# The reciprocal root of the first and of the last layer norm block begun from a ScalarE table function instead of a bit trick on VectorE

## The chip, the cores and the metric

The kernel runs on one core of a Trainium2 chip. The metric is device time in microseconds (us) of one execution, lower is better; several executions are timed and their median is the kernel's time. The engines are called by the profile's short names: PE (TensorE, matrix products), PEld (its weight loads), DVE (VectorE), ACT (ScalarE), POOL (GpSimd) and SP (SyncE, which here only issues DMAs). Each engine runs its own list of instructions in order; semaphores make one wait for another.

## The reference

Two decoder layers over 512 tokens of width 1024 in float32, with a layer norm ahead of the first layer. A layer projects its input, does sliding-window and sparse attention, projects back, adds and normalizes, then does a gated feed-forward network with a gated side input, adds and normalizes again.

```python
def layer_norm(x, g, b):
    mu = x.mean(-1, keepdims=True)
    var = jnp.square(x - mu).mean(-1, keepdims=True)
    return (x - mu) * lax.rsqrt(var + LN_EPS) * g + b

def reference(x, ...):
    x = layer_norm(x, ln_in_g, ln_in_b)
    for i in range(2):
        x = hybrid_layer(x, ...)
    return x

def hybrid_layer(x, ...):
    h = x @ w_in                       # queries, keys, values, indexer
    mix = concat(window_attention, sparse_attention) @ w_o
    x = layer_norm(DN_ALPHA * x + mix, ln1_g, ln1_b)
    g, u = jnp.split(x @ w_gu, 2, axis=-1)
    ffn = (jax.nn.silu(g) * u) @ w_down
    ple = (p_i @ w_pp) * jax.nn.sigmoid(x @ w_pg)
    return layer_norm(DN_ALPHA * x + ffn + ple, ln2_g, ln2_b)
```

## The kernel before

The 512 tokens lie in four blocks of 128 rows, tiles `x0` to `x3` (in the lists of instructions they are `x_85` to `x_88`). Products are made in three passes: every operand is split into a high and a low part, and `mm3` issues the three PE instructions of lines 325, 326 and 327. Weights come by DMA into `wst`, ACT copies the high part (line 278) and POOL subtracts for the low part (line 279); both parts lie in a `wsp` tile, of which there are five.

**The reciprocal root.** `rstd_of` gives 1/sqrt(var + eps) for the 128 rows of a block. All of it runs on DVE on tiles of 128x1: line 357 makes -0.5 times the variance (`lnv`), line 358 makes the first guess by integer arithmetic on the bits (`lns`), and lines 363 and 364 are a Newton step, done three times. Every block of every norm does this, and the small norm of the indexer keys too (on 128x2).

**The start.** Block 0 of the first norm is done by `ln_in(0)`: statistics on DVE (lines 372 and 392), the deviation from the mean times the gain (line 397, two halves), the root, and the product with it (line 400, two halves). `to_features(0)` then transposes the block on PE (line 438), ACT casts the two halves into the high part `fh` (line 440) and DVE subtracts for the low part `fl` (line 441); PE multiplies with the first weights. For blocks 1 to 3 ACT makes the sums (lines 382 and 383) and the squares (line 377), DVE the rest. ACT also makes part of the table of rotary angles (six and later four instructions of line 473, two sines in lines 481 and 482) and the casts of the weights. Line 562 begins, on DVE, the indexer norm of a block from its finished product.

**The end.** The last stage makes, for one block after the other, a sigmoid on ACT (line 1031), two DVE steps (lines 1032 and 1035), the mean (line 406), the squares on ACT (line 377, whose sum is read out by a second instruction), the deviation on DVE (line 418), the root, and the last product (line 422, for the last block in three pieces), each followed by its DMA to the output (line 423).

**What sets the order.** The instructions are written in program order by the functions below, but a scheduler then puts each engine's list in an order of its own, from estimates of when each will be ready, wherever data dependencies leave it free (`schedule_with_timeline_sim=True`). A function of ACT that needs another table makes the compiler put an ACT_TABLE_LOAD ahead of it.

Of the kernel before, what the change touches and what calls it, by code (L numbers as in the profile page):

```python
# [10 lines left out]
F32 = mybir.dt.float32  # L11
F32R = mybir.dt.float32r
BF16 = mybir.dt.bfloat16
I32 = mybir.dt.int32
AF = mybir.ActivationFunctionType
OP = mybir.AluOpType

L = 2
S = 512
D = 1024  # L20
NT = S // 128
# [8 lines left out]
EPS = 1e-5  # L30
# [66 lines left out]
def hybrid_kernel(ctx: ExitStack, tc: tile.TileContext, x, p, positions, ln_in_g, ln_in_b, w_in,  # L97
# [3 lines left out]
    PE, V, A, G, SP = nc.tensor, nc.vector, nc.scalar, nc.gpsimd, nc.sync  # L101

    const = ctx.enter_context(tc.tile_pool(name="const", bufs=1))
# [9 lines left out]
    def bank(tag, bufs, dt=F32):  # L113
        return psum.tile([128, 512], dt, name="bank", tag="bank", bufs=8)

    def acc():
        return bank("acc", 4)

    def slot(dt=F32R):
        return slots.tile([128, 512], dt, name="slot", tag="slot")  # L120

    def t2k(dt=F32):
        return tmp.tile([128, 512], dt, name="t2k", tag="t2k")

    def sm(n, name):
        return small.tile([128, n], F32, name=name, tag=name)
# [192 lines left out]
    def w_rel():  # L319
        wpos["room"] += 1  # L320
        w_pump()

    def mm3(o, sh, sl, mh, ml, start, stop, again=False):

        PE.matmul(o, sh, mh, start=start, stop=False, skip_group_check=again)  # L325
        PE.matmul(o, sh, ml, start=False, stop=False, skip_group_check=again)  # L326
        PE.matmul(o, sl, mh, start=False, stop=stop, skip_group_check=again)  # L327
# [20 lines left out]
    def tok(t):  # L348
        return slice(t * 128, (t + 1) * 128)


    def rstd_of(var, n=1, of=1):

        v = sm(n, f"lnv{n}")
        s = sm(n, f"lns{n}")
        t = sm(n, f"lnt{n}")
        V.tensor_scalar(v, var, of * EPS, -0.5 / of, op0=OP.add, op1=OP.mult)
        V.tensor_scalar(s.bitcast(I32), v.bitcast(I32), -0.5, float(0x5F3759DF - 2 ** 30 - 2 ** 22),
                        op0=OP.mult, op1=OP.add)
        for _ in range(3):  # L360
            for i in range(n):
                c = slice(i, i + 1)
                V.tensor_scalar(t[:, c], s[:, c], s[:, c], v[:, c], op0=OP.mult, op1=OP.mult)
                V.tensor_scalar(s[:, c], t[:, c], 1.5, s[:, c], op0=OP.add, op1=OP.mult)
        return s
# [3 lines left out]
    def ln_stats(t, h):  # L369
        if h == 0:  # L370
            stats[t] = small.tile([128, 2, 6], F32, name="bst", tag="bst")
        V.bn_stats(stats[t][:, h, :], xt[t][:, h * 512:(h + 1) * 512])

    def squares(t, nm):

        var = sm(1, "lnvar")
        last["squares"] = A.activation(t2k().bitcast(BF16), xt[t], AF.Square, bias=nm, accum_out=var).ins
        return var
# [7 lines left out]
    def ln_in(t):  # L386
        halves = [xt[t][:, h * 512:(h + 1) * 512] for h in range(2)]
        if t == 0:
            mv = sm(2, "bmv")
            for h in range(2):  # L390
                ln_stats(t, h)
            V.bn_aggr(mv, stats.pop(t))
            mean, var, of = mv[:, 0:1], mv[:, 1:2], 1
        else:
            (mean, var), of = stats.pop(t), D
        for h, c in enumerate(halves):
            V.scalar_tensor_tensor(c, c, mean, gb_in[h], op0=OP.add if t else OP.subtract, op1=OP.mult)
        rs = rstd_of(var, of=of)
        for h, c in enumerate(halves):
            last["norm"] = V.scalar_tensor_tensor(c, c, rs, gb_in[2 + h], op0=OP.mult, op1=OP.add).ins  # L400

    def ln_sums(t, sums, key, last_norm=False):

        g_t, b_t = gb[key]
        nm = sm(1, "lnm")
        V.tensor_scalar(nm, sums[:, 0:1], sums[:, 1:2], -1.0 / D, op0=OP.add, op1=OP.mult)
        var = squares(t, nm)
        if not last_norm:
            with tc.issue_after(last["norm"]) if t == NT - 1 else nullcontext():
                V.scalar_tensor_tensor(xt[t], xt[t], nm, g_t, op0=OP.add, op1=OP.mult)  # L410
            rs = rstd_of(var, of=D)
            last["norm"] = V.scalar_tensor_tensor(xt[t], xt[t], rs, b_t, op0=OP.mult, op1=OP.add).ins
            return
        dev = []
        for h in range(2):
            c = slice(h * 512, (h + 1) * 512)
            dev.append(slot(F32))
            V.scalar_tensor_tensor(dev[h], xt[t][:, c], nm, g_t[:, c], op0=OP.add, op1=OP.mult)
        rs = rstd_of(var, of=D)
        for c0, c1 in ((0, 512), (512, D)) if t < NT - 1 else ((0, 512), (512, 768), (768, D)):  # L420
            o = dev[c0 // 512][:, c0 % 512:c0 % 512 + c1 - c0]
            V.scalar_tensor_tensor(o, o, rs, b_t[:, c0:c1], op0=OP.mult, op1=OP.add)
            SP.dma_start(out[0, t * 128:(t + 1) * 128, c0:c1], o)
# [8 lines left out]
    def to_features(t):  # L432
        ts = slice(t * 128, (t + 1) * 128)
        for j in range(KT // 4):
            ps = bank("tp", 2)
            for i in range(4):
                k = 4 * j + i
                PE.transpose(ps[:, i * 128:(i + 1) * 128], xt[t][:, k * 128:(k + 1) * 128], idf)  # L438
            pv = ps.rearrange("p (a n) -> p a n", a=4)
            last["copy"] = A.copy(fh[:, 4 * j:4 * j + 4, ts], pv).ins  # L440
            V.tensor_tensor(fl[:, 4 * j:4 * j + 4, ts], pv, fh[:, 4 * j:4 * j + 4, ts], OP.subtract)  # L441
# [50 lines left out]

    w_pump()
    ln_in(0)
    table = rotary()
    next(table)
# [32 lines left out]
    def from_f(t, k):  # L529
        return fh[:, k, tok(t)], fl[:, k, tok(t)]  # L530

    def take(n):
        return [w_take() for _ in range(n)]
# [14 lines left out]
    for l in range(L):  # L548
# [231 lines left out]
        def res_out(h, scale, norm=None, stat=False):  # L780
            c = slice(h * 512, (h + 1) * 512)

            def f(t, ps):
                if stat:
                    if h == 0:
                        stats[t] = sm(2, "lnsum")
                    V.tensor_tensor_reduce(xt[t][:, c], ps, xt[t][:, c], 1.0, 0.0, op0=OP.add, op1=OP.add,
                                           accum_out=stats[t][:, h:h + 1])
                elif scale is None:
                    V.tensor_tensor(xt[t][:, c], ps, xt[t][:, c], OP.add)  # L790
                else:
                    V.scalar_tensor_tensor(xt[t][:, c], xt[t][:, c], scale, ps, op0=OP.mult, op1=OP.add)
                if norm is not None:
                    ln_sums(t, stats.pop(t), norm)
            return f
# [169 lines left out]
        for gi, fs in enumerate(GROUPS):  # L965
# [27 lines left out]
            for h in range(2):  # L993
                ps = [acc() for _ in range(NT)]
                n = len(hs)
# [13 lines left out]
        for b in TAIL:  # L1009
            for h in range(2):  # L1010
                if wg[h] is None:
                    wg[h] = take(5)
                ws = wg[h]
                c = slice(h * 512, (h + 1) * 512)
                ps = [acc() for _ in b]
                pq = [bank("sc", 2) for _ in b]
                for k in range(KT):
                    w = ws[k // 2]
                    for i, t in enumerate(b):
                        mm3(ps[i], *from_f(t, k), w[0][k % 2], w[1][k % 2], k == 0, k == KT - 1)  # L1020
                    if b is TAIL[-1] and h == 0 and k % 2 == 1:
                        w_rel()
                for k in range(2):
                    w = ws[4]
                    for i, t in enumerate(b):
                        mm3(pq[i], pT[k][0][:, tok(t)], pT[k][1][:, tok(t)], w[0][k], w[1][k], k == 0, k == 1)
                if b is TAIL[-1] and h == 0:
                    w_rel()
                for i, t in enumerate(b):
                    a = t2k()  # L1030
                    A.activation(a, ps[i], AF.Sigmoid)
                    V.tensor_tensor(a, pq[i], a, OP.mult)
                    if h == 0:
                        stats[t] = sm(2, "lnsum")
                    V.tensor_tensor_reduce(xt[t][:, c], xt[t][:, c], a, 1.0, 0.0, op0=OP.add, op1=OP.add,
                                           accum_out=stats[t][:, h:h + 1])
                    if h == 1:
                        ln_sums(t, stats.pop(t), ("2", l), l == L - 1)
            if l < L - 1 and b == (2,):
                to_features(0)  # L1040
                to_features(1)
# [26 lines left out]
```

## Time and profile before

| | |
|---|---|
| median of 3 runs | 1252.27 us (1252.04 to 1252.44) |
| the profiled execution | 1251.81 us |
| its span, first to last instruction | 1249.7 us |
| granted TensorE clock, mean | 0.998 |
| PE busy | 1225.9 us (98%) |
| DVE busy | 765.2 us (61%) |
| POOL busy | 682.9 us (55%) |
| ACT busy | 576.4 us (46%) |

The busy times overlap, since the engines run side by side. What an edit is worth is read in the stage where it stands: which engine is late there, and who waits for it. The chain of waits follows the program back from its last instruction, at each step to what released it.

### The profile page before, as it was taken

How to read it: one execution, taken by the hardware profiler on the slowest of the kernel's cores; microseconds unless marked ns; L12 is line 12 of the kernel's file. 1: busy time of each engine (PE TensorE's matmuls, PEld its weight loads, DVE VectorE, ACT ScalarE, POOL GpSimd, SP SyncE). 2: the span in 40 equal slices, each digit the busy share in tenths (PEclk: the TensorE clock that was granted, in tenths of full speed). 3: DMA queues.
4: the chain of work that ended last, by engine and by line, in shares of the span. 5: the costliest groups of instructions: out<-in, count | busy, mean ns of one | idle time of the engine just before them, and what ended most of it. 6: DMA issues, size and time to landing. Idle time of an engine off the chain costs nothing.

```text
span 1249.7 us, 18006 instructions
## 1 busy us (share of the span) xinstructions
PE 1225.9 (98%) x6552; PEld 1029.9 (82%) x6552; DVE 765.2 (61%) x1678; ACT 576.4 (46%) x1193; POOL 682.9 (55%) x555
## 2 busy tenths in 40 slices
PE   7999999999999999999999999999999999999996
PEld 5998777988888888888899987689888888888885
DVE  7699954682727272726677998286555555555365
ACT  6577763442434343433337787534343333333331
POOL 6885532566566666663169754234757575757400
PEclk9999999999999999999999999999999999999999
DMA  5232311333232323034033203114323333321321
GB/s 177 78 92 85 95 42 35 119 118 118 85 118 84 118 85 118 18 118 140 2 89 114 101 21 117 52 54 149 99 87 105 97 105 99 103 83 52 101 84 50
DMA packets 89264, 112.74 MB, mean 90 GB/s; under 512 B 5460, under 2 KB 66132, under 8 KB 89176
## 3 DMA queue, kind: packets, MB, share of 16 engines
q1 hardware_dynamic: 88504, 111.58, 28.5%
q8 instruction: 51, 0.84, 0.3%
q14 instruction: 37, 0.30, 0.1%
q10 hardware_dynamic: 672, 0.03, 0.0%
HBM read 109.49 MB, written 2.10 MB: 89 GB/s over the span
## 4 chain that ended last, share of the span: by engine, by line
PE 82%; POOL 5%; DVE 3%; issue 3%; ACT 3%; DMA 3%; SPq 0%; DVEq 0%; ACTq 0%; POOLq 0%
PE bank L325 24%; PE bank L326 24%; PE bank L327 24%; PE bank L715 3%; PE bank L684 3%; PE bank L721 2%; POOL wsp L279 2%; DMA wst<-in_w_pg_dram 2%; POOL wsp L257 1%; PE bank L523 1%; PE bank L438 1%; PE bank L732 1%; ACT wsp L278 1%; DVE slot L273 1%; POOL slot L517 1%
## 5 line engine op out<-in xcount | busy, mean ns | idle before, releaser
L279 POOL TENSOR_TENSOR wsp<-wst,wsp 128x1024 fp32r<-128x1024 f32 (+2 forms) x148 | 351.3, 2389 | 244.4 <-ACT wsp L278 240.8
L326 PE MATMUL bank<-fl,wsp 128*128 128x512 f32 (+1 forms) x768 | 284.8, 372 | 0.4 <-DVE fl L441 0.4
L325 PE MATMUL bank<-fh,wsp 128*128 128x512 f32 (+1 forms) x768 | 283.6, 372 | 1.0 <-ACT fh L440 1.0
L327 PE MATMUL bank<-fh,wsp 128*128 128x512 f32 (+1 forms) x768 | 283.1, 371 | 0.0
L278 ACT CAST wsp<-wst 128x1024 fp32r<-128x1024 f32 (+2 forms) x148 | 151.6, 1033 | 166.4 <-PE bank L327 126.2
L325 PE MATMUL bank<-wsp,fh 128*128 128x256 f32 (+3 forms) x512 | 165.2, 326 | 3.6 <-DVE work L648 2.0
L874 DVE TENSOR_TENSOR t2k<-bank,t2k 128x512 f32<-128x512 f32 x44 | 30.4, 692 | 222.0 <-PE bank L327 222.0
L326 PEld LDWEIGHTS bank<-fl,wsp 128*128 128x128 f32 x768 | 144.6, 188 | 25.7 <-DVE fl L441 0.9
L325 PEld LDWEIGHTS bank<-fh,wsp 128*128 128x128 f32 x768 | 143.6, 188 | 26.8 <-ACT fh L440 1.9
L327 PEld LDWEIGHTS bank<-fh,wsp 128*128 128x128 f32 x768 | 144.6, 188 | 24.9
L327 PE MATMUL bank<-wsp,fl 128*128 128x256 f32 (+3 forms) x512 | 163.7, 322 | 1.4 <-DVE fl L441 0.8
L326 PE MATMUL bank<-wsp,fh 128*128 128x256 f32 (+3 forms) x512 | 164.7, 322 | 0.0
L257 POOL TENSOR_TENSOR wsp<-slot,wsp 128x512 fp32r<-128x512 f32 x100 | 141.6, 1442 | 29.0 <-ACT wsp L256 29.0
L325 PE MATMUL bank<-wsp,slot 128*128 128x512 f32 x392 | 153.8, 392 | 0.0
L326 PE MATMUL bank<-wsp,slot 128*128 128x512 f32 x392 | 152.7, 390 | 0.0
L327 PE MATMUL bank<-wsp,slot 128*128 128x512 f32 x392 | 148.4, 390 | 0.0
L790 DVE TENSOR_TENSOR x<-bank,x 128x512 f32<-128x512 f32 x140 | 91.5, 684 | 88.5 <-PE bank L327 88.5
L904 ACT CAST slot<-t2k 128x256 fp32r<-128x256 f32 (+1 forms) x104 | 49.8, 497 | 144.1 <-DVE t2k L874 102.5
L257 POOL TENSOR_TENSOR wsp<-t2k,wsp 128x512 fp32r<-128x512 f32 x40 | 57.5, 1448 | 92.4 <-ACT wsp L256 92.4
L325 PEld LDWEIGHTS bank<-wsp,fh 128*128 128x128 f32 x512 | 97.6, 191 | 11.9 <-ACT fh L440 2.4
L327 PEld LDWEIGHTS bank<-wsp,fl 128*128 128x128 f32 x512 | 97.5, 191 | 7.9 <-DVE fl L441 1.1
L326 PEld LDWEIGHTS bank<-wsp,fh 128*128 128x128 f32 x512 | 98.0, 191 | 6.5 <-issue 1.2
(152 smaller groups left out, 2004.6 us busy)
## 6 DMA issues: line engine op xcount, KB each, us to landing
wst<-in_w_gu_dram SPq DMA_DIRECT2D x88, 512.0 KB, 3.5
slot<-in_w_down_dram SPq DMA_DIRECT2D x80, 256.0 KB, 2.8
wst<-in_w_in_dram SPq DMA_DIRECT2D x16, 512.0 KB, 3.6
wst<-in_w_o_dram SPq DMA_DIRECT2D x16, 512.0 KB, 3.8
wst<-in_w_pg_dram SPq DMA_DIRECT2D x16, 512.0 KB, 4.2
wst<-in_w_in_dram SPq DMA_DIRECT2D x8, 256.0 KB, 2.7
lng<-in_ln_g_dram SPq DMA_DIRECT2D x4, 512.0 KB, 4.8
lnb<-in_ln_b_dram SPq DMA_DIRECT2D x4, 512.0 KB, 5.5
```

The costliest lines, as they stand in the source:

```text
L257: G.tensor_tensor(w[:, 1, j], src[j], w[:, 0, j], OP.subtract)
L278: A.copy(w[:, 0, :a * n], st[:, :a * n])
L279: G.tensor_tensor(w[:, 1, :a * n], st[:, :a * n], w[:, 0, :a * n], OP.subtract)
L325: PE.matmul(o, sh, mh, start=start, stop=False, skip_group_check=again)
L326: PE.matmul(o, sh, ml, start=False, stop=False, skip_group_check=again)
L327: PE.matmul(o, sl, mh, start=False, stop=stop, skip_group_check=again)
L684: PE.matmul(ps[:, o:o + nn], qT[kind, t, g][:, j * 128:(j + 1) * 128], kT[c, s][:, k0:k0 + nn], start=(s == 0), stop=(s == 1))
L715: PE.matmul(o[u * 64:(u + 1) * 64], vt[b0 + b][:, c * 64:(c + 1) * 64], pts[b][:, u], start=b == 0, stop=b == nb - 1)
L721: PE.transpose(ps[:, j * 128:(j + 1) * 128], es[j][:, b * 128:(b + 1) * 128], idf)
L790: V.tensor_tensor(xt[t][:, c], ps, xt[t][:, c], OP.add)
L874: V.tensor_tensor(a, ps[1, f], a, OP.mult)
L904: A.copy(h[0], src)
```

## The change

A tile `tiny` holds eps in its first column. `rstd_of` gets an argument `table`: if it is set, ACT makes the first value from the variance by its function Abs_reciprocal_sqrt (with eps as the bias and the factor 1/of as the scale), in place of the bit trick on DVE, and two Newton steps follow in place of three. It is set for block 0 of the first norm (`ln_in`, t == 0) and for the last block of the last norm (`ln_sums` with `last_norm`, t == NT - 1). `load_root` calls the function on `tiny` alone, once ahead of everything and once in the source of the last stage, after the sigmoid of the last block's second half.

```diff
+    tiny = const.tile([128, 2], F32, name="tiny")
+    G.memset(tiny[:, :1], EPS)
+
+    def load_root():
+        A.activation(tiny[:, 1:], tiny[:, :1], AF.Abs_reciprocal_sqrt)
+
+    load_root()
+
-    def rstd_of(var, n=1, of=1):
+    def rstd_of(var, n=1, of=1, table=False):
...
         V.tensor_scalar(v, var, of * EPS, -0.5 / of, op0=OP.add, op1=OP.mult)
-        V.tensor_scalar(s.bitcast(I32), v.bitcast(I32), -0.5, float(0x5F3759DF - 2 ** 30 - 2 ** 22),
-                        op0=OP.mult, op1=OP.add)
-        for _ in range(3):
+        if table:
+            A.activation(s, var, AF.Abs_reciprocal_sqrt, bias=tiny[:, :1], scale=1.0 / of)
+        else:
+            V.tensor_scalar(s.bitcast(I32), v.bitcast(I32), -0.5, float(0x5F3759DF - 2 ** 30 - 2 ** 22),
+                            op0=OP.mult, op1=OP.add)
+        for _ in range(2 if table else 3):
...
-        rs = rstd_of(var, of=of)
+        rs = rstd_of(var, of=of, table=t == 0)
...
-        rs = rstd_of(var, of=D)
+        rs = rstd_of(var, of=D, table=t == NT - 1)
...
                     A.activation(a, ps[i], AF.Sigmoid)
+                    if l == L - 1 and t == NT - 1 and h == 1:
+                        load_root()
```

Line numbers below line 351 of the kernel before stand 9 to 13 higher in the changed kernel: its line 367 is the new ACT instruction, lines 374 and 375 are the Newton step (363 and 364 before), 393, 394, 388 and 451 are 382, 383, 377 and 440, 484 is 473, 524 and 528 are 513 and 517.

**ACT at the start.** Before, the list begins so; `x_86` is block 1:

```order
L473 ACT_TABLE_LOAD
L473 ACTIVATE t2k<-t2k 128x192 x6
L278 CAST wsp<-wst 128x888 x2
L382 ACTIVATE t2k,lnsum_192<-x_86 128x1024
L278 CAST wsp<-wst 128x592
L383 ACTIVATE lnm<-lnsum_192 128x1
L377 ACTIVATE t2k,lnvar<-x_86,lnm 128x1024
L440 CAST fh<-bank 128x4x128 x2
```

In the changed kernel:

```order
L356 ACT_TABLE_LOAD
L356 ACTIVATE tiny<-tiny 128x1 x2
L484 ACTIVATE t2k<-t2k 128x192 x6
L367 ACTIVATE lns_168<-bmv,tiny 128x1
L278 CAST wsp<-wst 128x888 x2
L393 ACTIVATE t2k,lnsum_193<-x_86 128x1024
L278 CAST wsp<-wst 128x592
L394 ACTIVATE lnm<-lnsum_193 128x1
L451 CAST fh<-bank 128x4x128
L388 ACTIVATE t2k,lnvar<-x_86,lnm 128x1024
L451 CAST fh<-bank 128x4x128
```

Both calls of `load_root` stand at the very start, the second one too; the first guess of block 0 stands behind the six angle instructions; and the first cast of block 0 stands ahead of the squares of block 1. There is one table load at the start, as before.

**ACT at the end.** Before, the list ends with these rows:

```order
L377 ACTIVATE t2k,lnvar<-x_86,lnm 128x1024
L1031 ACTIVATE t2k<-bank 128x512 x2
L377 ACTIVATE t2k,lnvar<-x_87,lnm 128x1024
L1031 ACTIVATE t2k<-bank 128x512 x2
L377 ACTIVATE t2k,lnvar<-x_88,lnm 128x1024
```

In the changed kernel:

```order
L388 ACTIVATE t2k,lnvar<-x_87,lnm 128x1024
L1042 ACTIVATE t2k<-bank 128x512 x2
L388 ACTIVATE t2k,lnvar<-x_88,lnm 128x1024
L367 ACT_TABLE_LOAD
L367 ACTIVATE lns_12021<-lnvar,tiny 128x1
```

A table load stands between the squares of the last block and the new instruction that reads them.

**POOL in the second layer,** where keys and values are turned (rows of rope, lines 513 and 517, among the weight subtractions of line 279). Before:

```order
L517 TENSOR_TENSOR slot<-t2k,slot 128x2x128
L513 TENSOR_TENSOR t2k<-t2k 128x64
L279 TENSOR_TENSOR wsp<-wst,wsp 128x1024
L517 TENSOR_TENSOR slot<-t2k,slot 128x128
L279 TENSOR_TENSOR wsp<-wst,wsp 128x1024
L513 TENSOR_TENSOR t2k<-t2k 128x2x64
L279 TENSOR_TENSOR wsp<-wst,wsp 128x1024 x2
L517 TENSOR_TENSOR slot<-t2k,slot 128x2x128
```

In the changed kernel:

```order
L528 TENSOR_TENSOR slot<-t2k,slot 128x2x128
L524 TENSOR_TENSOR t2k<-t2k 128x64
L528 TENSOR_TENSOR slot<-t2k,slot 128x128
L279 TENSOR_TENSOR wsp<-wst,wsp 128x1024 x3
L524 TENSOR_TENSOR t2k<-t2k 128x2x64
L279 TENSOR_TENSOR wsp<-wst,wsp 128x1024
L528 TENSOR_TENSOR slot<-t2k,slot 128x2x128
```

The rope step of 128x2x64 stands behind one more weight subtraction. The lists of the first layer's attention, of both feed-forward networks and of SP are as before; those of the second layer's attention are in a somewhat other order on PE, DVE, ACT and POOL.

## The prediction

> **What bounds the kernel now.** I read the busy shares of the page first, then the shares of the chain that ended last.
>
> ```profile
> PE 1225.9 (98%) x6552; PEld 1029.9 (82%) x6552; DVE 765.2 (61%) x1678; ACT 576.4 (46%) x1193; POOL 682.9 (55%) x555
> ...
> PE 82%; POOL 5%; DVE 3%; issue 3%; ACT 3%; DMA 3%; SPq 0%; DVEq 0%; ACTq 0%; POOLq 0%
> ```
>
> PE is busy for 1225.9 of 1249.7 us, so all that can be won without touching products is the 23.8 us in which PE has nothing, and these lie mostly at the two ends, where the change works. A difference of 0.2% (2.5 us) is about what a measurement of this kernel can tell from no change; the terms below are all smaller. Next I read the chain of waits over the first 45 us (start, length, engine and line):
>
> ```profile
> 7.53 1.63 ACT t2k L473 x6
> ...
> 12.57 1.25 ACT t2k L377 x2
> 13.85 1.40 DVE x L397 x2
> ...
> 15.97 0.61 PE bank L327
> ...
> 21.92 1.39 DVE x L397 x2
> ```
>
> The start is not set by block 0's root. The chain runs through ACT: the angles, the squares of block 1 until 13.82, then DVE's deviation of that block, which in DVE's list stands ahead of the low part (line 441) that block 0's first products wait for. Last, the timeline of the end shows the whole path from the last squares to the last product:
>
> ```profile
> 1242.97 0.18 ACT L377 ACTIVATION_READ_ACCUMULATOR t2k<-x,lnm 128x1 f32 x1
> 1243.19 0.15 DVE L357 TENSOR_SCALAR lnv<-lnvar 128x1 f32<-128x1 f32 x1
> 1243.37 0.15 DVE L358 TENSOR_SCALAR lns<-lnv 128x1 int32<-128x1 int32 x1
> 1243.56 0.27 DVE L363 TENSOR_SCALAR lnt<-lns,lnv 128x1 f32<-128x1 f32 x1
> ...
> 1244.12 0.27 DVE L363 TENSOR_SCALAR lnt<-lns,lnv 128x1 f32<-128x1 f32 x1
> ...
> 1245.24 1.54 DVE L422 SCALAR_TENSOR_TENSOR slot<-slot,lns,lnb 128x512 f32<-128x512 f32 x3
> ```
>
> Here nothing runs beside the root: every 0.1 us between 1243.15 (squares read out) and 1245.24 (line 422) is on the path. What leaves is line 358 (0.19 from its start to the next) and one step (0.56 between two starts of line 363), 0.75 together.
>
> **The end, costed.** What comes in its place depends on the table. The call of `load_root` after the last sigmoid does not stand there in the list of the changed kernel: both calls stand at the very start, and the table load is the row right behind the last squares. So I need the price of a load that stands between two ACT instructions:
>
> ```profile
> 90.22 0.41 ACT L516 CAST slot<-t2k 128x256 fp32r<-128x256 f32 x1 [0.25 <-POOL t2k L513]
> 90.65 1.28 ACT L692 ACT_TABLE_LOAD   x1
> 91.94 0.41 ACT L692 ACTIVATE t2k<-t2k,ng 128x128 f32<-128x128 f32 x1
> ```
>
> It begins 0.02 after the end of the one ahead (90.63), takes 1.28 and is followed after 0.01. The price of the new ACT instruction on 128x1 comes from other rows of ACT, at the start:
>
> ```profile
> 10.72 1.05 ACT L382 ACTIVATE t2k<-x 128x1024 bf16<-128x1024 f32 x1
> ...
> 12.34 0.20 ACT L383 ACTIVATE lnm<-lnsum 128x1 f32<-128x1 f32 x1
> 12.57 1.15 ACT L377 ACTIVATE t2k<-x,lnm 128x1024 bf16<-128x1024 f32 x1
> ...
> 20.88 0.19 ACT L377 ACTIVATION_READ_ACCUMULATOR t2k<-x,lnm 128x1 f32 x1
> ...
> 22.44 1.07 ACT L440 CAST fh<-bank 128x512 fp32r<-128x512 f32 x2 [0.37 <-PE bank L438]
> ```
>
> Line 383 takes 0.20 for this size. Line 377, which has a tile as its bias, takes 0.10 more than line 382, which has none, and the new one has such a bias: between 0.20 and 0.30, and I take 0.30, as the bias is known to be there. Then: the read-out ends 1243.15, load from 1243.17 to 1244.45, the guess from 1244.46 to 1244.76, 0.04 until DVE begins (as between the read-out and line 357), two steps of 0.56, and line 422 starts at 1245.92 in place of 1245.24. That is **+0.68** (0.58 with the short instruction). Line 357 needs only the variance and runs beside the load. Without the load the same sum would give 0.68 − 1.28 − 0.01 = −0.61; so the sign of this end hangs on that one row of the list. What follows line 422, its DMA, is as before.
>
> **The start, costed.** On DVE block 0 loses the same 0.75:
>
> ```profile
> 9.46 0.15 DVE L358 TENSOR_SCALAR lns<-lnv 128x1 int32<-128x1 int32 x1
> ...
> 11.38 1.41 DVE L400 SCALAR_TENSOR_TENSOR x<-x,lns,bank 128x512 f32<-128x512 f32 x2
> ...
> 21.80 0.20 DVE L562 BATCH_NORM_STATS2 kst<-bank 128x6 f32<-128x32 f32 x1 [0.45 <-PE bank L327]
> ...
> 23.50 0.66 DVE L441 TENSOR_TENSOR fl<-bank,fh 128x512 fp32r<-128x512 f32 x1
> 24.21 0.41 PE L327 MATMUL bank<-wsp,fl 128*128 128x296 f32 x1 [0.59 <-DVE lns L358]
> ```
>
> The new ACT instruction stands behind the six angles, so it runs from about 9.16 (7.53 + 1.63) to 9.46, no later than DVE was free for line 358, and line 400 can start near 10.65 in place of 11.38. The load is moved, not added, since there was one ahead of the angles already; the first call of `load_root` and the small memset lie before the angles' data are there. But what is won for block 0 has to pass ACT. The rows by windows (window, length, then busy time and count of PE, PEld, DVE, ACT and POOL, the clock, the DMA share, GB/s) say how full it is:
>
> ```profile
> 7.53:22.44 14.91, 11.91 (x42) 9.03 (x41) 12.52 (x35) 14.45 (x32) 14.06 (x14) 1.00 0.77 250
> 22.44:28.00 5.56, 4.73 (x35) 4.25 (x34) 5.56 (x24) 3.36 (x8) 3.68 (x9) 1.00 0.34 96
> ```
>
> ACT is busy for 14.45 of 14.91 us from the angles to the first cast of block 1 (line 440 at 22.44), and its only wait of size there is the 0.37 for PE ahead of this cast. It now also carries the new instruction, 0.2 net of overlap by its neighbours. With the wait gone the cast comes at 22.44 − 0.37 + 0.2 = 22.27, a gain of 0.17. That is the low end. The high end is DVE's: the list of DVE now has block 0's first low part ahead of block 1's deviation, so block 0's products end early and the 0.45 that DVE stood for them at 21.80 goes; the last block's squares end at 21.07 + 0.20 = 21.27, line 397 starts 0.04 behind them at 21.31, and line 441 comes 1.58 later (23.50 − 21.92) at 22.89 in place of 23.50. PE stood 0.59 for that row, so products of block 1 could run 0.6 sooner. From 22.44 to 28.00 DVE has no gap at all (5.56 of 5.56), so a shift there is handed on. Between 0.17 and 0.6 I take the middle, **−0.4**, since PE's first row of block 1 needs the cast (0.17) and its third the low part (0.6). Outer ends are −0.74, block 0's whole gain, and +0.2, if ACT's extra instruction is all that is left.
>
> **Between.** The scheduler also puts rows of the second layer's attention in another order. No instruction is added there, and I take 0. The bound below is all that PE waits in that stage, 621 to 835 us (waited-for row, then us, times, longest):
>
> ```profile
> PE bank L325 <- DVE work L648: 1.0, 1, 1.0
> PE bank L684 <- ACT slot L524: 0.8, 1, 0.8
> PE bank L325 <- ACT slot L613: 0.6, 1, 0.6
> PE bank L325 <- ACT fh L440: 0.5, 2, 0.2
> PE bank L715 <- ACT t2k L723: 0.2, 1, 0.2
> ```
>
> These sum to 3.1. The bound above is one weight step of POOL (line 279) by which a rotation (line 513) now stands further back:
>
> ```profile
> 670.39 0.45 POOL L513 TENSOR_TENSOR t2k<-t2k 128x128 f32<-128x128 f32 x1
> 670.80 4.78 POOL L279 TENSOR_TENSOR wsp<-wst,wsp 128x1024 fp32r<-128x1024 f32 x2
> 675.55 0.74 POOL L517 TENSOR_TENSOR slot<-t2k,slot 128x256 fp32r<-128x256 f32 x1
> ```
>
> Half of 4.78 is 2.39. The cover is that the consumer's last step, line 517, stood behind the fourth such step at 675.55 before and still does; if that cover fails, PE waits for the rotated keys. The first layer's attention has the same products and its lists keep their order but for two rows at its head.
>
> **Sum.** 1251.81 + 0.68 − 0.4 + 0 = 1252.09 for the profiled execution. The median of the runs stands 0.46 above that execution, so the time is 1252.27 + 0.28 = **1252.55**.
>
> **The rivals.** First, block 0's gain arrives whole at PE (−0.74) and the guess is short (+0.58): 1252.27 − 0.16 = 1252.1. For it speaks that PE waited 0.59 in the very place; against it, ACT's 14.45 of 14.91.
>
> Second, the load at the end holds ACT for longer than its row, because the engine must empty and settle around it as long again: +1.28, so 1253.8. For it: at the end the row ahead is a read-out whose result has only just been written. Against it: the load at 90.65 begins 0.02 behind its neighbour and ends 0.01 before the next. The Trainium skill, "ScalarE: Activation LUTs", section "What ACT_TABLE_LOAD costs", states some 1283 ns for the load and some 1380 ns of draining, 2.66 us for every switch; by that the time would be 1253.9. The trace agrees on the 1.28 and shows none of the rest.
>
> Third, on the other side: slower. In the second layer POOL does three weight steps before the rotation of the key block, PE's indexer products then wait the whole 2.39 for it, and nothing later takes it up, since PE is the bound: 1252.55 + 2.39 = 1254.9. It decides once PE's new wait passes 2.50 − 0.28 = 2.2 us. For it: POOL is the engine on the chain that follows PE in share (5%). Against: line 517 stays behind the fourth step.
>
> Fourth, faster: the new order of that attention takes all of PE's waits out, 1252.55 − 3.1 = 1249.5. Against it: five waits for five different rows would all have to go.
>
> That the change doesn't do what its source says is half settled by the list: the call near the end loads nothing there.
>
> **How the numbers follow.** The forecast has 0.61; block 0's whole gain 0.15; the long load 0.08; the late rotation 0.08; the waits gone 0.04; the remaining 0.04 are smaller shifts between these. All but the third and fourth lie within 0.2%, so same has 0.88, slower 0.08 and faster 0.04. Without the middle the ends are −0.74 + 0.58 and +0.2 + 0.68, 1252.1 to 1253.15, the forecast's own range. The range reaches above to the long load, rounded up, and below to 1252.1 with the longest of the second layer's waits (1.0) gone as well: 1251.1 to 1254.0.
>
> **What would show it.** At the end: a load of 1.28 right behind the last read-out, an ACT instruction of 0.2 to 0.3, two rows of line 363 and line 422 some 2.75 after the read-out. At the start: line 400 of block 0 near 10.65, block 1's cast near 22.3, PE's third pass of block 1 between 23.6 and 24.0. In the second layer: PE's waits still near 3 us. It is wrong if line 422 comes under 2.1 after the read-out (the load hidden), if the load has a gap of more than 0.1 on either side, or if PE gets a wait over 1 us in the second layer.

## Result and the profile after

The changed kernel takes 1268.13 us (median of 4 runs, 1266.97 to 1268.39) against 1252.15 for the kernel before (4 runs): +15.98 us, ratio 1.0126, 95% interval 1.0108 to 1.0143. The forecast was 1252.55, with a range of 1251.1 to 1254.0. The profiled execution took 1268.39, its span is 1266.5, 16.8 above that of before.

The page of the changed kernel, busy row and chain row:

```profile
PE 1240.8 (98%) x6552; PEld 1028.3 (81%) x6552; DVE 764.2 (60%) x1672; ACT 580.2 (46%) x1198; POOL 682.0 (54%) x556
...
PE 88%; ACT 4%; POOL 3%; DVE 2%; issue 2%; DMA 1%; ACTq 0%; DVEq 0%; SPq 0%; POOLq 0%
```

PE has as many instructions as before (6552) and is busy for 14.9 us longer. So most of the 16.8 us is not in a wait: PE does the same work more slowly. The groups by form say which part of the work (line, operation, tiles, shapes, count | busy, mean ns of one | idle ahead). Of the kernel before:

```profile
L326 PE MATMUL bank<-fl,wsp 128*128 128x512 f32 x640 | 249.0, 389 | 0.0
L326 PE MATMUL bank<-wsp,slot 128*128 128x512 f32 x392 | 152.7, 390 | 0.0
...
L326 PE MATMUL bank<-wsp,fh 128*128 128x512 f32 x128 | 49.8, 389 | 0.0
L326 PE MATMUL bank<-slot,fh 128*128 128x512 f32 x64 | 25.1, 393 | 0.3 <-DVE slot L273 0.2
```

Of the changed kernel:

```profile
L326 PE MATMUL bank<-fl,wsp 128*128 128x512 f32 x640 | 253.1, 396 | 0.0
L326 PE MATMUL bank<-wsp,slot 128*128 128x512 f32 x392 | 152.8, 390 | 0.0
...
L326 PE MATMUL bank<-wsp,fh 128*128 128x512 f32 x128 | 50.5, 395 | 0.0
L326 PE MATMUL bank<-slot,fh 128*128 128x512 f32 x64 | 25.5, 398 | 0.1
```

Every 512-wide product that takes one operand from `fh` or `fl` and the other from `wsp` or `slot` is 4 to 7 ns longer; those of `wsp` with `slot` are not. Lines 325 and 327 show the same. By the busy times of the three lines together, the 1920 products of `fh` or `fl` with 512 columns of `wsp` grew by 12.4 us, the 384 in which `wsp` is the other operand by 2.0 and the 192 of `slot` with `fh` or `fl` by 1.1, 15.5 us in all. The 256-wide ones became a little shorter (line 326: 286 before, 283 after), by 2.8 us in all. A slower clock or a busy neighbour would have to slow the products of `wsp` with `slot` as well, and it doesn't. What separates `fh` and `fl` from `wsp` and `slot` is on which side of the new tile they lie. `tiny` is allocated ahead of `tab64` and takes 32 bytes of each partition: in the compiled program `fh` starts at byte 17408 in both kernels, `wsp` at 99328 before and 99360 after, `slot` at 140288 and 140320.

The end, in the timeline of the changed kernel (the lines of before stand in the prediction):

```profile
1259.08 0.19 ACT L388 ACTIVATION_READ_ACCUMULATOR t2k<-x,lnm 128x1 f32 x1
1259.28 1.28 ACT L367 ACT_TABLE_LOAD   x1
...
1260.58 0.29 ACT L367 ACTIVATE lns<-lnvar,tiny 128x1 f32<-128x1 f32 x1
1260.91 0.27 DVE L374 TENSOR_SCALAR lnt<-lns,lnv 128x1 f32<-128x1 f32 x1 [1.46 <-ACT lns L367]
...
1262.02 1.54 DVE L433 SCALAR_TENSOR_TENSOR slot<-slot,lns,lnb 128x512 f32<-128x512 f32 x3
```

From the end of the read-out (1259.27) to the last product (line 433, 422 before) are 2.75 us, against 2.09: +0.66. The start, PE's timeline and then PE by windows (window, length, busy and count, granted clock, DMA share, GB/s):

```profile
18.16 0.29 PE L327 MATMUL bank<-wsp,fl 128*128 128x296 f32 x1
20.77 1.38 PE L449 MATMUL bank<-idf,x 128*128 128x128 f32 x8 [2.32 <-DVE x L411]
23.11 0.61 PE L325 MATMUL bank<-wsp,fh 128*128 128x296 f32 x1 [0.96 <-ACT fh L451]
...
59.76 1.13 PE L622 MATMUL bank<-idr,slot 128*128 128x128 f32 x12
```

```profile
20.00:25.00 5.00, 3.18 (x14) 0.77 0.55 145
25.00:30.00 5.00, 5.00 (x25) 0.54 0.13 46
```

Block 0's products now end by 18.45, PE waits 2.32 for block 1, and its granted clock is 0.77 and then 0.54 for the next ten microseconds. The row of line 622 (611 before, at 58.04 there) comes 1.72 late. The clock of the view does not tell all of it; the starts of the products tell more. Two products of block 0 and two of block 1 in the kernel before, then two of block 1 in the changed kernel:

```profile
19.59 0.45 PE L326 MATMUL bank<-wsp,fh 128*128 128x296 f32 x1
19.84 0.45 PE L327 MATMUL bank<-wsp,fl 128*128 128x296 f32 x1
...
25.00 0.30 PE L326 MATMUL bank<-wsp,fh 128*128 128x296 f32 x1
25.13 0.30 PE L327 MATMUL bank<-wsp,fl 128*128 128x296 f32 x1
```

```profile
25.07 0.45 PE L325 MATMUL bank<-wsp,fh 128*128 128x296 f32 x1
25.32 0.45 PE L326 MATMUL bank<-wsp,fh 128*128 128x296 f32 x1
```

At the slow pace they start 0.25 us apart, at the fast one 0.14. The kernel before takes all of block 0 at the slow pace, where the view has a granted clock of 1.00 (the prediction's window to 22.44 shows it), and block 1 at the fast one. The changed kernel reaches the fast pace within block 0, at 15.94, and falls back for the whole of block 1.

### The profile page after: what moved, and what is told of

Its sections match the earlier page's. It is cut to its first block, busy times and chain, and to the rows that moved or that the text cites. A ratio compares the mean times of both kernels' runs of the same rounds, so it can differ in the third digit from the quotient of the medians.

```text
span 1266.5 us, 18011 instructions
## 1 busy us (share of the span) xinstructions
PE 1240.8 (98%) x6552; PEld 1028.3 (81%) x6552; DVE 764.2 (60%) x1672; ACT 580.2 (46%) x1198; POOL 682.0 (54%) x556
## 4 chain that ended last, share of the span: by engine, by line
PE 88%; ACT 4%; POOL 3%; DVE 2%; issue 2%; DMA 1%; ACTq 0%; DVEq 0%; SPq 0%; POOLq 0%
PE bank L325 26%; PE bank L326 26%; PE bank L327 26%; PE bank L695 3%; PE bank L726 3%; PE bank L732 2%; POOL wsp L279 1%; DMA wst<-in_w_pg_dram 1%; ACT wsp L278 1%; PE bank L534 1%; POOL slot L528 1%; PE bank L449 1%; PE bank L743 1%; PE bank L656 0%; POOL t2k L524 0%
## 5 line engine op out<-in xcount | busy, mean ns | idle before, releaser
L326 PE MATMUL bank<-fl,wsp 128*128 128x512 f32 (+1 forms) x768 | 288.8, 377 | 0.4 <-DVE fl L452 0.4
L325 PE MATMUL bank<-fh,wsp 128*128 128x512 f32 (+1 forms) x768 | 287.6, 377 | 1.0 <-ACT fh L451 1.0
L327 PE MATMUL bank<-fh,wsp 128*128 128x512 f32 (+1 forms) x768 | 287.0, 376 | 0.0
```

## Experiments

Three theories stood at the beginning. A: a product is slower when its two operands lie at different offsets within some period. B: the loss comes from the instructions, the tables and the order. C: a tile at 32 within 64 bytes is slow by itself. The kernels of e1, e3, e4, e7, e8 and e9 have each engine's list of before row for row; only addresses differ.

**e1: the 32 bytes alone**

```diff
+    pad = const.tile([128, 2], F32, name="pad")    # where tiny stands, unused
```

> The kernel before with one unused tile of 128x2 in the place where the change has `tiny`: it takes 32 bytes of each partition, so every tile that is allocated behind it (the weight tiles wst and wsp, slot, t2k) lies 32 bytes higher, and fh, fl and x lie where they were. No instruction is added or moved. Theory A (the products slow down because one operand lies at 0 and the other at 32 bytes within 64): +14 us over before, about 1266.5, with the 512-wide products of fh or fl with wsp at 0.232 to 0.235 us apart in place of 0.227, and those of wsp with slot at 0.227. Theory B (the loss comes from the moved instructions, the root and the tables): 1252.2, no difference. Theory C (each tile at 32 within 64 is slow for itself): slower too, with the products of wsp and slot slow as well.

Measured: 1265.89, ratio 1.011 (1.0094 to 1.0127), +13.8 us. Its row for the 640 products:

```profile
L326 PE MATMUL bank<-fl,wsp 128*128 128x512 f32 x640 | 253.4, 396 | 0.0
```

An unused tile costs 13.8 of the 16.0 us that the change costs. B falls for the bulk.

**e2: `tiny` of 64 bytes, in the changed kernel**

```diff
-    tiny = const.tile([128, 2], F32, name="tiny")
+    tiny = const.tile([128, 16], F32, name="tiny")
```

> The changed kernel with `tiny` 16 columns wide (64 bytes) in place of 2; the engines' lists are the same row for row. Theory A: all tiles are back at 0 within 64, the 512-wide products run 0.227 apart again, and what is left over before is the start (about +1.8, read from the trace of the changed kernel) and the end (+0.66): about 1254.7. Theory B: 1268, as the changed kernel. Theory C: as A.

Measured: 1266.19, ratio 1.011 (1.0095 to 1.0125). I had taken the period for 64 bytes, and that was wrong: 64 bytes are nearly as bad as 32.

```profile
L326 PE MATMUL bank<-fl,wsp 128*128 128x512 f32 x640 | 252.6, 395 | 0.0
```

**e3: the 32 bytes ahead of everything**

```diff
+    pad = const.tile([128, 2], F32, name="pad")    # unused
     fh = const.tile([128, KT, S], F32R, name="fh")
```

> The kernel before with the unused 128x2 tile allocated ahead of fh, so that fh, fl, x, the weight tiles and the slots all lie at 32 within 64. No instruction is added or moved. Theory A (only a difference between the two operands counts): 1252.2, no slowing. Theory C (32 within 64 is slow for itself): slower by 14 us or more, as in the padded kernel, with wsp-by-slot products slow too. Theory B: 1252.2.

Measured: 1252.33 beside 1252.12, ratio 1.0003 (0.9993 to 1.0012).

```profile
L326 PE MATMUL bank<-fl,wsp 128*128 128x512 f32 x640 | 249.2, 389 | 0.0
```

All operands lie at 32 within 64 here, and nothing is slow. C falls: it is the difference between the operands that counts.

**e4: the 32 bytes between `wsp` and `slot`**

```diff
+    padp = ctx.enter_context(tc.tile_pool(name="padp", bufs=1))
     slots = ctx.enter_context(tc.tile_pool(name="slots", bufs=NSLOT))
...
+    pad = padp.tile([128, 2], F32, name="pad")     # unused
```

> The kernel before with the unused 128x2 tile allocated between the weight tiles and the slots: fh, fl, wsp at 0 within 64, slot and t2k at 32. No instruction is added or moved. Theory A: now the 1176 products of wsp with slot (and the 192 of slot with fh and fl) run at 0.232 to 0.235, those of fh with wsp at 0.227: +8 to +10 us, about 1261. Theory C, in the form that the weight tiles' address alone decides: 1252.2. Theory B: 1252.2.

Measured: 1259.18, ratio 1.0055 (1.004 to 1.007), +7.1 us, just under what A said.

```profile
L326 PE MATMUL bank<-fl,wsp 128*128 128x512 f32 x640 | 249.3, 390 | 0.0
L326 PE MATMUL bank<-wsp,slot 128*128 128x512 f32 x392 | 155.0, 395 | 0.0
...
L326 PE MATMUL bank<-slot,fh 128*128 128x512 f32 x64 | 25.4, 397 | 0.0
```

The slow group has changed sides: `wsp` with `slot` is now at 395 ns in place of 390, and `fl` with `wsp` is as in the kernel before. This is theory A's own sign.

**e7, e8, e9: the period**

```diff
 e7:  ikg and ikb (512 bytes) allocated behind fl instead of ahead of fh
 e8:  an unused tile of 128x32 (128 bytes) where tiny stands
 e9:  ikb alone (256 bytes) behind fl
```

> The kernel before with ikg and ikb allocated behind fl in place of ahead of fh: fh and fl lie 512 bytes lower, everything else (x, wsp, slots) where it was. Lists the same row for row. If the offset between the operands counts modulo 512 or a divisor of it: 1252.1. If modulo 1024 or more: products of fh and fl with wsp at 0.232 to 0.235, +13 to +15 us; products of wsp with slot unchanged.

> The kernel before with an unused tile of 128x32 (128 bytes) in the place of `tiny`: wsp and slots 128 bytes off fh. Lists the same row for row. Offset counted modulo 128: 1252.1. Modulo more than 128: +13 to +15 us, near 1266.

> The kernel before with ikb alone allocated behind fl: fh and fl lie 256 bytes lower, everything else (x, wsp, slots) where it was, lists the same row for row. An offset of 512 cost nothing, one of 128 cost 15 us. If 256 is harmless: 1252.0. If only multiples of 512 are harmless: 1265 to 1267, products of fh and fl with wsp at 0.230 to 0.235.

Measured: e7 (offset 512) 1252.15, ratio 1.0001 (0.9992 to 1.001); e8 (128) 1267.32, ratio 1.0121 (1.0106 to 1.0137); e9 (256) 1251.96, ratio 0.9999 (0.999 to 1.0008). The row of the 640 products in e7, e8 and e9:

```profile
L326 PE MATMUL bank<-fl,wsp 128*128 128x512 f32 x640 | 249.0, 389 | 0.0
...
L326 PE MATMUL bank<-fl,wsp 128*128 128x512 f32 x640 | 252.6, 395 | 0.0
...
L326 PE MATMUL bank<-fl,wsp 128*128 128x512 f32 x640 | 249.0, 389 | 0.0
```

Offsets of 32, 64 and 128 bytes cost 12 to 15 us in this kernel, 256 and 512 nothing.

**e5: the change without its shift**

```diff
+    tinyp = ctx.enter_context(tc.tile_pool(name="tinyp", bufs=1))   # the last pool
-    tiny = const.tile([128, 2], F32, name="tiny")
+    tiny = tinyp.tile([128, 2], F32, name="tiny")
```

> The changed kernel with `tiny` in a pool of its own behind all others, so that no tile lies elsewhere than in the kernel before; the engines' lists are those of the changed kernel row for row. The run with 64 bytes left the 512-wide products slow, so the offset has to be a multiple of more than 64 to be harmless, or the theory of two operands at different offsets is wrong. Theory A (relative offset, with a period over 64): products 0.227 apart again, what remains is the start and the end as read from the changed kernel's trace, 1.8 + 0.66 over before, about 1254.7. Theory B (the instructions): 1266 to 1268.

Measured: 1253.66 (11 runs, 1252.76 to 1254.48) beside 1251.92, ratio 1.0012 (1.0004 to 1.0021), +1.7 us. With the lists of the changed kernel, the products of `fl` with `wsp` are at 389 again. Of the 16.0 us, about 14.2 (15.98 − 1.74, each kernel beside its own runs of before) were the addresses; the instructions cost the other 1.7. It came out 1.0 under my 1254.7. The likely reason is that in the execution that I had read the start from, PE's clock was down; in the one profiled here, 0.8 under the median of its runs, it isn't. PE by windows and PE's timeline in e5:

```profile
20.00:25.00 5.00, 2.89 (x18) 1.00 0.56 153
25.00:30.00 5.00, 4.35 (x36) 1.00 0.10 35
```

```profile
20.79 1.38 PE L449 MATMUL bank<-idf,x 128*128 128x128 f32 x8 [1.53 <-DVE x L411]
23.12 0.40 PE L325 MATMUL bank<-wsp,fh 128*128 128x296 f32 x1 [0.96 <-ACT fh L451]
...
58.06 1.13 PE L622 MATMUL bank<-idr,slot 128*128 128x128 f32 x12
...
616.28 1.91 PE L449 MATMUL bank<-idf,x 128*128 128x128 f32 x16
...
829.63 1.03 PE L449 MATMUL bank<-idf,x 128*128 128x128 f32 x8
```

The wait for block 1 was 1.53, 36 instructions ran from 25 to 30 us in place of 25, and line 622 comes at 58.06 (line 611 at 58.04 before). Two single executions can't be compared that closely by their absolute times: in kernels whose lists begin alike, the first angle instruction of ACT starts anywhere from 7.53 (before) to 8.66 (e3), since POOL, whose result it needs, waits 2.48 us (before) to 3.54 us (e3) for a DMA. Counted from that instruction, line 622 comes after 50.18 in e5; in the eight kernels that start as before (before, e1, e3, e4, e6 to e9) its counterpart comes after 49.92 to 50.52, in the changed kernel after 51.91. So in e5 nothing of the root's shorter chain can be told from that spread. Between the transposes ahead of the second layer's attention and those behind it lie 213.35 us. In the kernel before:

```profile
616.21 1.91 PE L438 MATMUL bank<-idf,x 128*128 128x128 f32 x16
...
829.05 1.03 PE L438 MATMUL bank<-idf,x 128*128 128x128 f32 x8
```

That is 212.84; the new order there costs 0.51. It shows in PE's waits of e5 from 590 to 850 us (us in all, times, longest):

```profile
PE bank L325 <- ACT slot L624: 0.7, 1, 0.7
...
PE bank L726 <- ACT t2k L734: 0.5, 2, 0.3
```

They were 0.6 and 0.2.

**e6: the end alone, with the preload held in its place**

```diff
-                    A.activation(a, ps[i], AF.Sigmoid)
+                    sg = A.activation(a, ps[i], AF.Sigmoid).ins
                     if l == L - 1 and t == NT - 1 and h == 1:
-                        load_root()
+                        with tc.issue_after(sg): load_root()
```

with `tiny` in the last pool, the first call of `load_root` left out and block 0 as in the kernel before.

> The kernel before with the table function for the last block alone, `tiny` behind all other tiles, and the preload held behind the last sigmoid, so that the table load stands ahead of the last squares where ACT waits 2.54 us. The lists of PE and SP are those of before, DVE loses one row of the bit trick and one step. From the sum of the prediction without the load: line 422 starts 0.61 earlier, 1251.5. Rival: the load delays the squares or the guess waits on something else, and nothing or less than 0.2 is won: 1252.1.

Measured: 1251.15 beside 1251.92 (11 and 27 runs), ratio 0.9994 (0.9985 to 1.0003): 0.8 by the medians, not clear of zero by its interval. The timeline shows it directly:

```profile
1239.22 1.28 ACT L356 ACT_TABLE_LOAD   x1
...
1241.75 1.15 ACT L388 ACTIVATE t2k<-x,lnm 128x1024 bf16<-128x1024 f32 x1 [1.02 <-DVE lnm L417]
1242.80 0.19 ACT L388 ACTIVATION_READ_ACCUMULATOR t2k<-x,lnm 128x1 f32 x1
...
1243.02 0.29 ACT L367 ACTIVATE lns<-lnvar,tiny 128x1 f32<-128x1 f32 x1
...
1244.46 1.54 DVE L433 SCALAR_TENSOR_TENSOR slot<-slot,lns,lnb 128x512 f32<-128x512 f32 x3
```

The load lies in ACT's wait for the mean, which shrinks to 1.02, and from the read-out's end (1242.99) to the last product are 1.47 us: 0.62 less than before.

**e10, e11, e12: PE filled at the start, both ends, all together**

```diff
 e10: the kernel of e5, and ahead of block 1's transposes, behind block 0's last product:
+            for _ in range(fill if j == 0 else 0):     # 24 for block 1
+                with tc.issue_after(last["mm"]): PE.transpose(ps[:, :128], xt[0][:, :128], idf)
...
 e11: the kernel of e5 with load_root held behind the last sigmoid, as in e6
 e12: e10 and e11 together
```

> The changed kernel with `tiny` behind all other tiles, as measured at 1253.66, and 24 more transposes of block 0's first 128 columns on PE between block 0's last product and block 1's transposes (they write into the bank that block 1's transposes then overwrite). They take about 2.6 us cold, 1.5 to 2.6 warm, in the 1.5 to 2.3 us that PE waits there. Theory (PE's clock falls back in that wait in some executions): the slow executions go, the runs spread less than 1 us, and since the scheduler's order of the second layer is here that of the kernel before, some 0.5 more goes: 1252.2. Rival (the wait doesn't matter to the clock): 1253.1 with the same spread of 1.7 us, or more where the transposes delay block 1.

> The changed kernel with `tiny` behind all other tiles and the second call of load_root held behind the last sigmoid, so that the table load at the end stands in ACT's wait of 2.54 us. PE's, DVE's and POOL's lists are those of the changed kernel. From the two runs: 1253.66 less the 0.66 lost at the end and less the 0.77 won by the pinned preload: 1252.2. If the two ends are not additive, up to 1253.

> All three mends: tiny behind all other tiles, the preload held behind the last sigmoid, and PE filled in its wait for block 1. If the terms add: 1252.2 - 1.4 = 1250.8, the fastest of all. If the table at the start is worth nothing: as the kernel with the pinned end alone, 1251.15.

Measured, each with 11 runs beside 1251.81: e10 1251.81 (1251.34 to 1252.66), ratio 1.0 (0.9991 to 1.0008); e11 1252.72 (1252.09 to 1253.51), ratio 1.0007 (0.9998 to 1.0016); e12 1250.60 (1250.06 to 1251.08), ratio 0.9989 (0.998 to 0.9998). The terms nearly add: e10 is 1.74 under e5, each beside its own runs of before (1.85 by the plain medians), e12 2.1 under e11. e10's runs spread 1.3 us, more than the 1.0 that I gave, less than e5's 1.7; the 33 runs of the kernel before spread 1.7 too, so the spread decides nothing. Adding the transposes also put the second layer's order back to that of before, and its stretch with it. PE's timeline of e10:

```profile
19.75 2.78 PE L448 MATMUL bank<-idf,x 128*128 128x128 f32 x24
22.36 1.04 PE L451 MATMUL bank<-idf,x 128*128 128x128 f32 x8
...
616.47 1.91 PE L451 MATMUL bank<-idf,x 128*128 128x128 f32 x16
...
829.31 1.03 PE L451 MATMUL bank<-idf,x 128*128 128x128 f32 x8
```

212.84 again. So 0.5 of the 1.74 is that order; the other 1.2 fits the clock, but no kernel kept the order of e5 with PE filled, so the share is worked out and not shown alone. Counted from the first angle instruction, the counterpart of line 611 comes after 49.77 in e10 and 49.80 in e12, earlier than in any kernel that starts as before, if only just. e12 is the only kernel here whose ratio has its interval wholly below 1.

## Why the prediction was wrong

**The step that failed** is the costing of `tiny` in "The start, costed". It was priced by its memset only, which did run before anything waited for it (on POOL at 1.36); that the tile stands ahead of the weight tiles and moves their addresses had no term, so it was put at nothing without a reason, and none of the four rivals had that mechanism. The measured size of the missing term is 13.8 us alone (e1) and about 14.2 within the change (e5 against the changed kernel). The trace of before could hardly price it, since `fh`, `wsp` and `slot` start multiples of 1024 bytes apart there; but the new `const` tile was in the diff, and its place could be read. None of the three signs of being wrong that the prediction names came up: they look at the end and at PE's waits in the second layer, and the loss was in the pace of PE's own products.

**The end** was right: +0.68 forecast, +0.66 measured, with the load, the guess at 0.29 and two steps as summed. What the same sum gives without the load, −0.61, was measured too: −0.62 in e6. The rival of a load that holds ACT for twice its row is gone: 0.01 from the read-out's end to the load, 0.02 from the load's end to the guess.

**The start** had the right path and the wrong sign. In the changed kernel the angles began 0.32 later (7.85, not 7.53), by the spread of that DMA. Counted from them, block 1's first cast came 0.26 earlier (at 22.50; 0.17 was forecast) and PE's third pass of block 1 0.61 earlier (at 23.92; 0.6 was forecast). What failed was "products of block 1 could run 0.6 sooner": ending block 0 early lengthened PE's wait, and PE then took block 1's products at the slow pace. In the profiled execution that made line 622 1.72 late. In medians the start's part in e5 is what is left over, 1.7 − 0.66 − 0.51, some 0.6 lost. With PE filled it is a gain: e10 less the 0.66 of the end leaves −0.7, e12 (1.21 under its runs of before) less e6's 0.77 leaves −0.4. That is near the −0.4 of the forecast, but each of these differences is smaller than its interval, about 1 us to either side.

**Between** was taken as 0 and is +0.51, inside its bounds (−3.1 to +2.39). The rival of a whole weight step is gone: no wait of PE in that stage grew by more than 0.3. So is the rival with the waits gone: they all stayed. The sentence that the first layer's lists keep their order but for two rows was too strong: on PE some products at its head are in another order too.

## What to carry to other kernels

Before an unused-looking line is priced at nothing, ask what it moves in memory: here a tile of 32 bytes per partition in an early pool cost 13.8 us, and the best arrangement of the whole change (e12) won 1.2. Put new small tiles into the last pool, or keep big operands of a product a multiple of 256 bytes apart. Look for signs of being wrong in the pace of the busiest engine too, and not in its waits alone. Hold a preload to its neighbour explicitly, since here the scheduler moved it to the start of the list; and before work is pulled ahead of a gap, ask whether the engine keeps its clock through it.

## What the runs showed of the hardware

A product of 512 columns is 3 to 7 ns slower when its stationary and its moving operand start 32, 64 or 128 bytes apart modulo 256 (e1, e2, e8), and not when they start 256 or 512 apart (e7, e9) or lie 32 bytes higher together (e3). In the kernel before such products start 227 ns apart (median), so this is up to 3%. The 256-wide ones are not slower (286 and 283 ns). No other offset was run. Why is open; no run separated the reading of one operand from that of the other.

PE's pace fell back to the slow one after a wait of 2.32 us in the changed kernel (granted clock 0.77 and 0.54 from 20 to 30 us) and stayed fast after one of 1.53 in the same lists (e5); in e11, after 2.04, the clock was 0.90 and 0.76 in the same two windows. The Trainium skill, "TensorE: Matmul & The Clock Gate", section "What's actually happening", says that the clock is halved after an idle window of about 3.4 us and that the window runs freely, so the moment differs between executions. The differing moments agree with these traces: block 0's products reach the fast pace at 15.94 in the changed kernel, at 18.14 in e5 and at 17.14 in e11. No single wait here is as long as that window; behind the 2.32 come 1.38 us of transposes and another wait of 0.96, and no run shows how much of this was needed.
